# A two-layer diffusion backbone on one core: the context stream goes first in layer 0, and one token tile of the latent stream takes gathered experts there

## The chip, the core and the metric

The kernel runs on one core of a Trainium2 chip. The number that counts is the device time of one execution in microseconds (us). The core has five engines with instruction queues of their own: TensorE (PE in the profile; its weight loads, PEld, overlap its matmuls), VectorE (DVE), ScalarE (ACT), GpSimd (POOL) and SyncE (SP). Each queue runs strictly in its own order. Transfers between main memory and the on-chip buffers are issued from SP, ACT and POOL and share 16 DMA engines.

## The reference

Two layers work on 512 latent tokens (`x`) and 256 context tokens (`ctx`), width 1024. The context goes through the whole of layer 0; in layer 1 only its keys and values are used.

```python
for l in range(DEPTH):                                   # DEPTH = 2
    xn = modulate(rms_norm(h, norm1_g[l]), mod[:, 0], mod[:, 1])
    cn = modulate(rms_norm(hc, norm1_g[l]), mod_c[0], mod_c[1])
    ...
    o = blocked_diff_attn(q, concat([k, kc]), concat([v, vc]), lam)        # x attends to x and ctx
    mix = mixer_output(o, p, ...)                        # gates * (attention, pooling, short conv) @ w_out
    if not last:
        oc = diff_attn_core(qc, kc, vc, lam)             # ctx attends to ctx
        hc = hc + mod_c[2] * mixer_output(oc, pc, ...)
    h = h + mod[:, 2] * mix
    h = h + mod[:, 5] * peer_ffn(modulate(rms_norm(h, ...)), ...)
    if not last:
        hc = hc + mod_c[5] * peer_ffn(modulate(rms_norm(hc, ...)), ...)

def peer_ffn(x, ...):                                    # 16384 experts of one neuron each
    s1, i1 = top_k(scores of the first half key, 16); s2, i2 = top_k(second half, 16)
    top_s, eidx = the best 16 of the 256 sums, for each of 8 heads
    hid = gelu(einsum('td,thkd->thk', x, u_emb[eidx]))
    return einsum('thk,thkd->td', softmax(top_s) * hid, v_emb[eidx])
```

So each token picks 8 x 16 = 128 experts and needs 128 rows of `u_emb` and 128 of `v_emb`.

## The kernel before

A token tile is 128 tokens: `x` has four, `ctx` has two. Float32 products are made of three matmuls on split operands (`mm3`, lines 97 to 100): every weight that arrives from memory is split by ScalarE (line 93) and VectorE (line 94) into a high and a low part. `load_w` brings a projection's weights in pieces of 512 KB (`wraw`, `whi`, `wlo`).

The experts are evaluated in two ways. **Dense**: all 16384 experts for a block of tokens. `hidden` streams the whole of `u` (tiles `uraw`, `uh`, `ul`; 128 of them in a layer, each with 24 matmuls into `hid`), `weigh` multiplies with a gate matrix `G` that `gates` has made (zero where an expert was not picked; `gA`, `gB`, `gE`), and `values` streams the whole of `v` (`vraw`, `vh`, `vl`; again 128 tiles, 24 matmuls each into `dps`, then an addition to `acc`). The matmuls' width is the number of dense tokens. **Gathered**: for one token tile, `gathered` (line 840) fetches the picked rows, one of 128 x 1024 numbers at a time, 256 in all: an indirect DMA issued by POOL (line 846), then one VectorE operation of that size: a dot product with the token's input `gx` for a `u` row (line 859), a weighted addition to `gacc` for a `v` row (line 869). TensorE has no part in it. The rows share a few buffers (tag `row`), so POOL issues the next one when VectorE has used the oldest.

In layer 0 both `ctx` tiles are gathered and all four `x` tiles are dense (width 512); in layer 1 one `x` tile is gathered and three are dense (width 384). `trunk` writes layer 0 in this order: queries, keys and values of both streams (`qkv`), attention of `ctx` and then of `x` (`attend`, `head`), the rest of `ctx` (pooling, convolution, gates, output projection), the pooling of `x`, then `ctx_ffn` with the choice of experts for `ctx` and its gathered rows, and then the rest of `x`. A scheduler at build time sets the order on every engine from the written order and a priority; `prio` shifts it, and the gathered rows carry a shift of 40000, that is, they fill what is left. `head` needs for each head of `x` the loads `hq`, `hk`, `hkl`, `hv`, which POOL's queue issues too, and on VectorE the softmax (`mx`, `at`) and the split `tl` of the transposed weights, on which the matmul into `po` waits.

## Time and profile before

| what | value |
|---|---|
| median of 3 runs | 5148.17 us (5141.2 to 5151.72) |
| the profiled execution, device time | 5138.01 us |
| its span, first to last instruction | 5136.2 us |
| PE busy | 4934.7 us (96%) |
| DVE busy | 3946.9 us (77%) |
| ACT busy | 1988.4 us (39%) |
| POOL busy | 1180.5 us (23%) |
| moved by DMA | 1280.77 MB, mean 249 GB/s |

A share over the whole span is an average of stages with different limits. The profile is therefore read by stretches: for each, how long it took, how much of it each engine was busy, and the share and rate of the DMA engines. In the trace the first gathered row of layer 0 is used at 1092 us, its first dense `u` tile is split at 1335 us, its first `v` tile at 2100 us, its last gathered row at 2953 us, and layer 1's own work begins at about 3010 us.

### The profile page before, as it was taken

What the parts mean: (1) busy time and instruction counts of PE and PEld (TensorE: products, weight loads), DVE (VectorE), ACT (ScalarE), POOL (GpSimd) and SP (SyncE); (2) the same over time, 40 slices, a digit from 0 to 9 for tenths busy, and PEclk for the clock granted to TensorE, in tenths of its full rate; (3) what the DMA queues carried; (4) which work ended last, traced back from release to release, by engine and by line L of the source; (5) the groups of instructions that cost most, each with busy time, mean ns of one, the idle gap of its engine ahead of it and who ended that gap; (6) DMA issues with size and microseconds to landing.
All of it is one profiled execution on the core that took longest, in us unless ns stands there. A gap on an engine that the chain in (4) does not pass through costs nothing.

```text
span 5136.2 us, 73940 instructions
## 1 busy us (share of the span) xinstructions
PE 4934.7 (96%) x27373; PEld 4195.8 (82%) x27373; DVE 3946.9 (77%) x7993; ACT 1988.4 (39%) x2968; POOL 1180.5 (23%) x1028
## 2 busy tenths in 40 slices
PE   8999999998899999989999999999999999899999
PEld 5688787776688788768888789777679999899999
DVE  5457676697899998568888867666359999787885
ACT  4346664422333344222233234544334344332333
POOL 0001000024433343333333300000000434344320
PEclk9999999999999999999999999999999999999999
DMA  8667453468897889999999845533355888988995
GB/s 305 239 200 224 137 191 108 155 200 273 302 316 259 285 312 339 329 321 326 336 341 344 311 137 166 161 126 97 109 172 174 277 309 331 330 314 294 329 317 177
DMA packets 509035, 1280.77 MB, mean 249 GB/s; under 512 B 42496, under 2 KB 224640, under 8 KB 500352
## 3 DMA queue, kind: packets, MB, share of 16 engines
q1 hardware_dynamic: 302816, 669.35, 38.5%
q0 software_dynamic: 131968, 449.90, 25.7%
q10 hardware_dynamic: 73888, 156.79, 8.1%
q8 instruction: 215, 3.52, 0.3%
q14 instruction: 148, 1.21, 0.1%
HBM read 1098.13 MB, written 177.73 MB: 248 GB/s over the span
## 4 chain that ended last, share of the span: by engine, by line
PE 64%; DMA 14%; DVE 11%; issue 7%; POOL 2%; ACT 1%; SPq 0%; ACTq 0%; POOLq 0%; DVEq 0%
PE mm L98 6%; DMA row<-peer_v,ix 6%; PE mm L100 6%; PE mm L99 6%; DMA row<-peer_u,ix 6%; PE dps L99 5%; PE dps L100 5%; PE dps L98 5%; PE hid L100 4%; PE hid L98 4%; PE hid L99 4%; PE qk L98 3%; PE qk L100 3%; PE qk L99 2%; POOL row L846 2%
## 5 line engine op out<-in xcount | busy, mean ns | idle before, releaser
L100 PE MATMUL hid<-yh,ul 128*128 128x512 f32 (+1 forms) x2048 | 760.2, 372 | 33.9 <-DVE ul L94 33.6
L98 PE MATMUL hid<-yh,uh 128*128 128x512 f32 (+1 forms) x2048 | 757.1, 370 | 21.0 <-ACT yh L286 13.2
L846 POOL DMA_INDIRECT row<-peer_v,ix x384 | 568.5, 1480 | 876.7 <-DVE gacc L869 501.1
L846 POOL DMA_INDIRECT row<-peer_u,ix x384 | 521.4, 1358 | 1059.7 <-DVE row L859 617.7
L99 PE MATMUL hid<-yl,uh 128*128 128x512 f32 (+1 forms) x2048 | 755.7, 369 | 2.3 <-DVE yl L287 2.3
L98 PE MATMUL dps<-wh,vh 128*128 128x512 f32 (+1 forms) x2048 | 735.1, 365 | 20.0 <-ACT vh L93 18.6
L99 PE MATMUL dps<-wl,vh 128*128 128x512 f32 (+1 forms) x2048 | 741.7, 365 | 12.3 <-DVE wl L94 12.3
L100 PE MATMUL dps<-wh,vl 128*128 128x512 f32 (+1 forms) x2048 | 742.0, 364 | 10.4 <-DVE vl L94 10.4
L98 PE MATMUL mm<-hi,whi 128*128 128x512 f32 (+1 forms) x1856 | 666.5, 360 | 12.3 <-DVE y L582 3.1
L100 PE MATMUL mm<-hi,wlo 128*128 128x512 f32 (+1 forms) x1856 | 660.6, 358 | 14.0 <-DVE wlo L94 14.0
L99 PE MATMUL mm<-lo,whi 128*128 128x512 f32 (+1 forms) x1856 | 662.4, 357 | 3.5 <-DVE lo L94 3.5
L859 DVE SCALAR_TENSOR_TENSOR row<-row,gx 128x1024 f32<-128x1024 f32 x384 | 467.0, 1221 | 170.3 <-DMA row<-peer_u,ix 169.5
L869 DVE SCALAR_TENSOR_TENSOR gacc<-row,gw,gacc 128x1024 f32<-128x1024 f32 x381 | 488.1, 1281 | 133.7 <-DMA row<-peer_v,ix 132.6
L94 DVE TENSOR_TENSOR wlo<-wraw,whi 128x1024 fp32r<-128x1024 f32 (+1 forms) x356 | 427.2, 1202 | 179.6 <-ACT whi L93 177.2
L93 ACT ACTIVATE uh<-uraw 128x1024 fp32r<-128x1024 f32 x256 | 271.5, 1061 | 716.4 <-PE hid L99 651.9
L93 ACT ACTIVATE whi<-wraw 128x1024 fp32r<-128x1024 f32 (+1 forms) x356 | 370.5, 1043 | 404.4 <-PE mm L99 305.2
L93 ACT ACTIVATE vh<-vraw 128x1024 fp32r<-128x1024 f32 x256 | 270.2, 1058 | 641.9 <-PE dps L99 395.1
L100 PEld LDWEIGHTS hid<-yh,ul 128*128 128x128 f32 x2048 | 390.2, 191 | 82.9 <-DVE ul L94 44.6
L98 PEld LDWEIGHTS hid<-yh,uh 128*128 128x128 f32 x2048 | 391.1, 191 | 64.1 <-ACT yh L286 15.6
L98 PEld LDWEIGHTS dps<-wh,vh 128*128 128x128 f32 x2048 | 386.7, 189 | 61.9 <-ACT vh L93 19.4
L99 PEld LDWEIGHTS dps<-wl,vh 128*128 128x128 f32 x2048 | 387.1, 189 | 54.8 <-DVE wl L94 14.4
L100 PEld LDWEIGHTS dps<-wh,vl 128*128 128x128 f32 x2048 | 387.2, 189 | 51.5 <-DVE vl L94 11.1
(332 smaller groups left out, 9480.4 us busy)
## 6 DMA issues: line engine op xcount, KB each, us to landing
uraw<-uT SPq DMA_DIRECT2D x256, 512.0 KB, 5.7
vraw<-v SPq DMA_DIRECT2D x256, 512.0 KB, 6.8
wraw<-w_in SPq DMA_DIRECT2D x216, 512.0 KB, 4.4
gd<-gst ACTq DMA_DIRECT2D x28, 2048.0 KB, 10.7
mw<-w_mod SPq DMA_DIRECT2D x96, 512.0 KB, 7.0
wraw<-wq SPq DMA_DIRECT2D x80, 512.0 KB, 6.0
hidd<-ge ACTq DMA_DIRECT2D x128, 256.0 KB, 5.6
G<-gd SPq DMA_DIRECT2D x32, 1024.0 KB, 10.7
```

Source lines behind the costliest of these rows:

```text
L93: self.nc.scalar.activation(hi, src, AF.Copy)
L94: self.nc.vector.tensor_tensor(lo, src, hi.bitcast(F32), op=OP.subtract)
L98: mm(ps, lh, rh, start=start, stop=False)
L99: mm(ps, lh, rl, start=False, stop=False)
L100: mm(ps, ll, rh, start=False, stop=stop)
L846: nc.gpsimd.indirect_dma_start(out=r, out_offset=None, in_=a[t], in_offset=bass.IndirectOffsetOnAxis(ap=idx[:, s:s + 1], axis=0))
L859: nc.vector.scalar_tensor_tensor(out=r, in0=r, scalar=1.0, in1=x, op0=OP.mult, op1=OP.mult, accum_out=hid[:, k:k + 1])
L869: nc.vector.scalar_tensor_tensor(acc, r, w[:, k:k + 1], acc, op0=OP.mult, op1=OP.add)
```

## The change

It has five parts.

1. **One tile of `x` is gathered in layer 0 too** (`self.gath = (1, 1)`). The dense block there has 384 tokens instead of 512, three tiles' gate matrices are built instead of four, and 256 more rows are fetched, with a priority of their own (`late[0] = (1000, 28)`: 1000, and 28 more for each row). Their sum goes to memory (`natx`), and `gather_end` transposes and adds it when the dense values are done.
2. **`ctx` first.** `trunk0` writes attention, branches, output projection and expert choice of `ctx` before the attention of `x`. The pooling and convolution of `x` follow its attention.
3. **The rows' sums of `ctx` are added late.** They go to memory (`natc`), and layer 1 (`trunk1`, `begin`) reads them back, adds them, and makes the norm, keys and values of `ctx` after the pooling of `x`. `qkv` is called for `x` and for `ctx` apart, so in layer 1 the weights of keys and values are loaded and split twice (16 pieces of 512 KB more).
4. **Buffers.** Four row buffers instead of three; one instead of two for each of `hv`; five `at` in layer 0 instead of six; two `nt` in a norm with `nat`; the keys in four pieces; three instead of four `vh` and `vl` in the mixed stage of layer 1.
5. The merge of the convolution's output with the gates is a step of its own (`v`, then `o`), and `gx` stays on chip instead of going through memory.

```diff
-    def attend(self, l, es, parts, side=None):
+    def attend(self, l, es, parts, side=None, ahead=2):
...
-                v = [ap_.tile([P, nk, P], F32R, tag=f"hv{x}", name=f"hv{x}") for x in range(2)]
+                v = [ap_.tile([P, nk, P], F32R, tag=f"hv{x}", name=f"hv{x}", bufs=1) for x in range(2)]
...
-            at = ap_.tile([P, nk * P], F32, tag="a", name="at", bufs=6)
+            at = ap_.tile([P, nk * P], F32, tag="a", name="at", bufs=na)
...
-            r = gp.tile([P, D], F32, tag="row", name="row", bufs=3)
+            r = gp.tile([P, D], F32, tag="row", name="row", bufs=self.rows)
...
+                with self.prio(late[0] + n * late[1]):
+                    r = fetch("peer_u", h * 16 + k)
+                    nc.vector.scalar_tensor_tensor(out=r, in0=r, scalar=1.0, in1=x, op0=OP.mult, op1=OP.mult,
+                                                   accum_out=hid[:, k:k + 1])
+                n += 1
...
+    def gather_end(self, l, nat, c, n, i, gp, gq, h):
...
+        nc.sync.dma_start(h, self.hmid[l][:, c:c + n].rearrange("(k p) t -> p k t", p=P))
+        for t in range(n // P):
+            acc = gp.tile([P, D], F32, tag="gend", name="gend", bufs=1)
+            nc.sync.dma_start(acc, nat[t * P:(t + 1) * P, :])
+            self.gather_add(l, acc, i, gq, h[:, :, t * P:(t + 1) * P])
...
+        self.rows = 4
...
+        self.gath, self.late = (1, 1), ((1000, 28), (40000, 0))
...
-            self.qkv(l, [X, Cx], "kqv")
-            if l == 0:
-                self.attend(l, ea, [(Cx, XT, CT), (X, 0, TT)], "right")
-                with ExitStack() as e2:
-                    hc = self.mixers(l, Cx, self.pool(e2, "fc", 2, PSUM), cp, "pcgo")
-                with ExitStack() as e2, self.prio(4000):
-                    self.pooling(l, [X], self.pool(e2, "fp", 2, PSUM))
-                ea.close()
-                ges = self.ctx_ffn(l, hc)
-                ec.close()
-                with ExitStack() as e2:
-                    hm = self.mixers(l, X, self.pool(e2, f"fl{l}", 3, PSUM), xp, "gco")
...
+        self.qkv(0, [X, Cx], "kqv")
+        with ExitStack() as ea, ExitStack() as e2:
+            self.attend(0, ea, [(Cx, XT, CT)], "right")
+            hc = self.mixers(0, Cx, self.pool(e2, "fc", 2, PSUM), cp, "pckvgo")
+        self.ctx_ffn(0, hc, cp, gpools)
+        ec.close()
+        with ExitStack() as ea, ExitStack() as e2:
+            self.attend(0, ea, [(X, 0, TT)], "right", 1)
+            hm = self.mixers(0, X, self.pool(e2, "fl0", 2, PSUM), xp, "pc|kvgo", ea)
...
+        self.qkv(1, [X], "kqv")
...
+        def begin():
+            ges.close()
+            with ExitStack() as ec:
+                self.parts(ec, "xc1", Cx)
+                self.load_norm(1, Cx, lambda h, hp, es: self.gather_end(0, self.natc, NX, NC, 1, hp, self.pool(es, "gq", 1, PSUM), h))
+                self.qkv(1, [Cx], "kv")
+            self.attend(1, ea, [(X, 0, TT)], "right")
...
-        nd = XT if l == 0 else XT - 1
+        nd = XT - self.gath[l]
...
-                        self.values(l, n, cs, self.weigh(l, n, va, cs, had), lambda dq: (vb, 3, vb, EC + 2), vq, acc, c == S + EC)
+                        self.values(l, n, cs, self.weigh(l, n, va, cs, had), lambda dq: (vb, 3, vb, EC + 1), vq, acc, c == S + EC)
```

What the scheduler makes of it is seen in the queues. First VectorE, layer 0, the last head of the attention of `x`; `tl` is the split on which TensorE waits, `row` and `gacc` are gathered rows. Before:

```order
L94 TENSOR_TENSOR tl<-tr_6283,th 128x512
L94 TENSOR_TENSOR wlo<-wraw,whi 128x512
L527 TENSOR_TENSOR psum_9637<-pu 128x527
L527 TENSOR_TENSOR psum_9639<-psum_9637 128x525
L527 TENSOR_TENSOR psum_9641<-psum_9639 128x521
L530 TENSOR_TENSOR psum_9641<-psum_9641,edge 128x4
L532 TENSOR_TENSOR psum_9641<-psum_9641,edge 128x3
L535 SCALAR_TENSOR_TENSOR pd<-psum_9641,pu 128x512
L94 TENSOR_TENSOR pl<-pd,ph 128x512
L94 TENSOR_TENSOR tl<-tr_6295,th 128x512
```

After:

```order
L443 SCALAR_TENSOR_TENSOR at<-p,rcx,at 128x768
L875 SCALAR_TENSOR_TENSOR gacc<-row,gw,gacc 128x1024
L94 TENSOR_TENSOR tl<-tr_11925,th 128x512
L875 SCALAR_TENSOR_TENSOR gacc<-row,gw,gacc 128x1024 x3
L94 TENSOR_TENSOR tl<-tr_11937,th 128x512
L875 SCALAR_TENSOR_TENSOR gacc<-row,gw,gacc 128x1024 x2
L862 SCALAR_TENSOR_TENSOR row,ghid<-row,gx_7555 128x1024
L94 TENSOR_TENSOR tl<-tr_11949,th 128x512
L862 SCALAR_TENSOR_TENSOR row,ghid<-row,gx_7555 128x1024 x3
L94 TENSOR_TENSOR tl<-tr_11961,th 128x512
```

Before, no gathered row stood in the attention; after, three stand ahead of each split.

Second POOL's queue, in the same part of layer 0, the loads for the heads of `x`. Before:

```order
L408 DMA hk<-kd_65 128x1536
L406 DMA hq<-qd_63 128x2x512
L410 DMA hkl<-ld_67 128x768
L413 DMA hv_5116<-vd_69 128x768
L413 DMA hv_5117<-vd_69 128x768
```

After:

```order
L408 DMA hk<-kd_65 128x1536
L406 DMA hq<-qd_63 128x2x512
L410 DMA hkl<-ld_67 128x768
L849 DMA row<-peer_u,ix_8621 128x1024 x16
L849 DMA row<-peer_v,ix_8621 128x1024 x4
L413 DMA hv_10770<-vd_69 128x768
L413 DMA hv_10771<-vd_69 128x768
L849 DMA row<-peer_v,ix_8621 128x1024 x2
```

The fetches of rows and the heads' loads now stand in one another's way.

Third VectorE in layer 0's stage of dense values. Before:

```order
L869 SCALAR_TENSOR_TENSOR gacc<-row,gw,gacc 128x1024
L94 TENSOR_TENSOR vl<-vraw,vh 128x1024
L800 TENSOR_TENSOR gel<-gel,G 128x512 x4
L869 SCALAR_TENSOR_TENSOR gacc<-row,gw,gacc 128x1024
L94 TENSOR_TENSOR vl<-vraw,vh 128x1024
L859 SCALAR_TENSOR_TENSOR row,ghid<-row,gx 128x1024
L94 TENSOR_TENSOR wl<-gel,wh 128x512
L831 TENSOR_TENSOR acc<-dps,acc 128x512
```

After:

```order
L94 TENSOR_TENSOR vl<-vraw,vh 128x1024 x2
L875 SCALAR_TENSOR_TENSOR gacc<-row,gw,gacc 128x1024 x2
L835 TENSOR_TENSOR acc<-dps,acc 128x384
L875 SCALAR_TENSOR_TENSOR gacc<-row,gw,gacc 128x1024 x2
L835 TENSOR_TENSOR acc<-dps,acc 128x384
L875 SCALAR_TENSOR_TENSOR gacc<-row,gw,gacc 128x1024
L94 TENSOR_TENSOR wl<-gel,wh 128x384 x4
L875 SCALAR_TENSOR_TENSOR gacc<-row,gw,gacc 128x1024 x2
```

About two rows go with each value tile in place of one to two, and the other operations are narrower.

## Rows read from the trace of the kernel before

**Rows 1.** The page's head: span, then busy time of each engine
```profile
span 5136.2 us, 73940 instructions
PE 4934.7 (96%) x27373; PEld 4195.8 (82%) x27373; DVE 3946.9 (77%) x7993; ACT 1988.4 (39%) x2968; POOL 1180.5 (23%) x1028
```

**Rows 2.** The page's 40 slices: VectorE's busy tenths, then GB/s moved
```profile
DVE  5457676697899998568888867666359999787885
GB/s 305 239 200 224 137 191 108 155 200 273 302 316 259 285 312 339 329 321 326 336 341 344 311 137 166 161 126 97 109 172 174 277 309 331 330 314 294 329 317 177
```

**Rows 3.** Busy time by stretch: ends, length, engines, clock, DMA share, GB/s
```profile
core 0: us, PE busy (x) PEld busy (x) DVE busy (x) ACT busy (x) POOL busy (x), PEclk, DMA share, GB/s
...
350.00:1092.00 742.00, 723.27 (x4105) 591.07 (x4105) 545.64 (x1406) 399.87 (x657) 60.78 (x160) 0.97 0.52 165
1092.00:1335.00 243.00, 213.89 (x891) 168.39 (x889) 186.65 (x242) 64.43 (x80) 107.62 (x93) 0.98 0.83 282
1335.00:2100.00 765.00, 737.79 (x4346) 615.77 (x4346) 691.28 (x1625) 289.23 (x439) 270.49 (x184) 0.98 0.86 304
2100.00:2953.00 853.00, 826.37 (x3601) 680.15 (x3601) 699.22 (x905) 247.66 (x318) 316.97 (x241) 0.98 0.94 329
2953.00:3010.00 57.00, 50.60 (x196) 36.13 (x195) 35.74 (x57) 21.47 (x35) 0.00 (x0) 0.92 0.53 166
3010.00:5136.00 2126.00, 2048.76 (x11985) 1869.54 (x11984) 1605.92 (x3226) 836.22 (x1241) 420.83 (x339) 0.98 0.66 226
1372.00:1991.00 619.00, 605.13 (x3617) 510.85 (x3618) 587.31 (x1484) 231.19 (x354) 218.37 (x154) 0.99 0.86 300
2600.00:2900.00 300.00, 300.00 (x1324) 248.14 (x1323) 265.19 (x355) 88.75 (x112) 111.24 (x87) 1.00 0.98 343
```

**Rows 4.** The same view for `dps` (512 wide, 384 wide) and `qk` (256 wide)
```profile
2300.00:2900.00 600.00, 600.00 (x2647) 496.61 (x2647) 76.42 (x112) 1.00 0.97 338
4800.00:5100.00 300.00, 298.73 (x1714) 296.27 (x1713) 38.92 (x72) 1.00 0.83 288
3060.00:3200.00 140.00, 133.01 (x1069) 129.21 (x1069) 14.60 (x22) 12.54 (x21) 1.00 0.47 152
```

**Rows 5.** VectorE's groups by line and shape: count, busy us, mean ns, idle before
```profile
L869 DVE SCALAR_TENSOR_TENSOR gacc<-row,gw,gacc 128x1024 f32<-128x1024 f32 x381 | 488.1, 1281 | 133.7 <-DMA row<-peer_v,ix 132.6
L859 DVE SCALAR_TENSOR_TENSOR row<-row,gx 128x1024 f32<-128x1024 f32 x384 | 467.0, 1221 | 170.3 <-DMA row<-peer_u,ix 169.5
...
L94 DVE TENSOR_TENSOR ul<-uraw,uh 128x1024 fp32r<-128x1024 f32 x256 | 311.9, 1219 | 47.6 <-ACT uh L93 47.6
...
L831 DVE TENSOR_TENSOR acc<-dps,acc 128x512 f32<-128x512 f32 x120 | 82.0, 686 | 20.7 <-PE dps L100 20.7
...
L743 DVE TENSOR_TENSOR gB<-gE,sl 128x1024 f16<-128x1024 f16 x112 | 76.7, 686 | 5.4 <-PE gps L751 5.2
...
L831 DVE TENSOR_TENSOR acc<-dps,acc 128x384 f32<-128x384 f32 x120 | 65.9, 554 | 33.0 <-PE dps L100 33.0
```

**Rows 6.** Waits of POOL: line, releaser, us in total, times, longest
```profile
POOL row L846 <- DVE row L859: 773.5, 291, 16.5
...
POOL hv L413 <- PE po L100: 191.3, 19, 48.6
```

**Rows 7.** Timeline at the first rows: a fetch, its use, the buffer's next fetch
```profile
1088.58 1.39 POOL L846 DMA_INDIRECT row<-peer_u,ix  x1 [0.30 <-issue]
...
1095.82 1.23 DVE L859 SCALAR_TENSOR_TENSOR row<-row,gx 128x1024 f32<-128x1024 f32 x1 [1.39 <-DMA row<-peer_u,ix]
...
1097.32 1.21 POOL L846 DMA_INDIRECT row<-peer_u,ix  x1 [2.08 <-DVE row L859]
```

**Rows 8.** All uses of `row`, 1080 to 1335 us and 2100 to 2960 us: landing
```profile
DMA to landing us min/median/max: 4.4/6.1/9.2
...
DMA to landing us min/median/max: 4.1/7.1/11.8
```

More of the change, by code (lines that the diff above doesn't have):

```diff
@@ L213, in rotary @@
         nc.sync.dma_start(rows, bass.AP(tensor=r.tensor, offset=r.offset + 384 * l, ap=[[0, P], [1, 2 * HD]]))
+        gains = [rows[:, off:off + HD] for off in (R_QG, R_KG)]
+        if not turn:
+            return None, None, gains
         cs = pool.tile([P, XT, 2, 32], F32, name="cs")
@@ L224, in rotary @@
                                                g[:, 1 - s][:, None].to_broadcast([P, XT, 32]), op0=OP.mult, op1=OP.mult)
-        gains = [rows[:, off:off + HD] for off in (R_QG, R_KG)]
         return rc, rs, gains
@@ new lines, in gathered @@
+        if end is None:
+            with self.prio(late[0] + n * late[1]):
+                nc.sync.dma_start(out, acc)
+        else:
+            end(acc)
+    def gather_end(self, l, nat, c, n, i, gp, gq, h):
+        nc = self.nc
+        nc.sync.dma_start(h, self.hmid[l][:, c:c + n].rearrange("(k p) t -> p k t", p=P))
[3 more added lines that the diff above has]
+            self.gather_add(l, acc, i, gq, h[:, :, t * P:(t + 1) * P])
@@ L880, in load_norm, with gather_add @@
+    def gather_add(self, l, acc, i, gq, h):
+        tr = gq.tile([P, 4, P], F32, tag="gtr", name="gtr", bufs=1)
+        for k in range(KT):
+            self.nc.tensor.transpose(tr[:, k % 4], acc[:, k * P:(k + 1) * P], self.ident)
+            self.nc.vector.scalar_tensor_tensor(h[:, k], tr[:, k % 4], self.modT[l][:, 40 + k, i:i + 1], h[:, k], op0=OP.mult, op1=OP.add)
+    def load_norm(self, l, s, load, between=None, side=None):
         with ExitStack() as es:
@@ L973, in mixers @@
+    def mixers(self, l, s, pp, xp, order, attn=None, begin=None):
         z, m, gates = Stream(s.o, s.n, s.i), Stream(s.o, s.n, s.i), []
@@ L1013, in gather, with gather_out @@
         nc.vector.tensor_copy(gk, g)
-        dst = self.hout if l == 0 else self.out
-        self.gathered(l, [(rows, ix, gk, self.hmid[l][:, cols], i, dst[:, cols])], gp, gq, self.natd[l], late)
+        self.gathered(x, out, ix, gk, gp, late, end)
+    def gather_out(self, gp, gq, acc, c):
+        col = lambda d: d[:, c].rearrange("(k p) t -> p k t", p=P)
+        h = gp.tile([P, KT, P], F32, tag="row", name="gres", bufs=self.rows)
+        self.nc.sync.dma_start(h, col(self.hmid[DEPTH - 1]))
+        self.gather_add(DEPTH - 1, acc, 0, gq, h)
+        self.nc.sync.dma_start(col(self.out), h)
     def ranks(self, mp):
```

261 lines of the change are left out of this document (128 added, 133 removed).

## The prediction

> **What bounds the kernel now.** I read the page's head first: TensorE is busy 96% of the span, VectorE 77% [rows 1]. That alone says that less TensorE work means less time. The slices say where it may not be so: VectorE and the DMA engines are loaded very unevenly [rows 2]. So I went by stretches [rows 3]. In layer 0 from the first dense tile on, three resources are near full at once: from 1335 to 2100 us VectorE is busy 691 of 765 us, and in its densest part (1372 to 1991) 587 of 619, or 95%; from 2100 to 2953 the DMA engines are at a share of 0.94 and 329 GB/s, in the fullest 300 us at 0.98 and 343 GB/s. In layer 1 (3010 to 5136) the shares are 76% of VectorE and 0.66 of the DMA engines. TensorE sets the pace, but in layer 0 by a small margin. The row fetches use up that margin: VectorE sits 134 and 170 us before the two row operations, nearly always for the row's landing [rows 5], and POOL waits 773 us for VectorE to release a row buffer [rows 6].
>
> **The change, part by part.** The sum is made against the profiled execution: span 5136.2 us, device time 5138.0; the median of the runs is 10 us above that.
>
> TensorE's saving. The 6144 dense matmuls of layer 0 go from 512 to 384 columns. In the stages of pure `dps` work one took 600/2647 = 0.2267 us at 512 and 300/1714 = 0.1750 at 384 [rows 4]. 6144 x 0.0517 = 318 us. If TensorE stayed the bound, that would be the gain.
>
> What it costs. 256 more rows of (488.1 + 467.0)/765 = 1.25 us on VectorE [rows 5] are 320 us. Against that stand narrower operations (554 in place of 686 ns; 128 each of two kinds, and about 128 additions: 51 us) and a quarter of layer 0's gate building (64 operations of 686 ns: 44 us). VectorE gains 225 us of work and TensorE loses 318, all in layer 0. The DMA engines get 256 x 0.524 = 134 MB more and some 34 MB less (gates and hidden values of a fourth tile).
>
> Layer 0 must therefore be summed with all three resources. I count along VectorE's order in the changed kernel, with the mean durations of the groups.
>
> *Until the first gathered row.* Queries, keys and values end at about 350 us as before. Then comes `ctx` alone: 2112 projection matmuls of 256 columns at 0.125 us (between 0.131, which holds some transposes, of [rows 4], and half of 0.2267) are 264 us; its eight heads and norms some 40; the choice of experts and the waits in this chain, which the attention of `x` no longer fills at each step, 100 (no row shows the chain alone; between 50, a little over what 742 us of elapsed time for 723 busy lose [rows 3], and 140). First row at 760 instead of 1092 us.
>
> *Trunk of `x` with rows* (299 of them before the first dense tile is split). VectorE's work other than rows from 350 to 1335 was 546 + 187 - 86 x 1.25 = 625 us [rows 3]; about 300 of it is now ahead of the first row, 310 remain. With 299 x 1.25 = 373 that is 683 us of VectorE for about 505 of TensorE: VectorE bounds. At its best 95% this takes 719 us. A second limit is near: a buffer was fetched at 1088.58, used at 1095.82 and fetched again at 1097.32 [rows 7], 8.74 us for one round, so four buffers give a row every 2.2 us, 299 in 653 us. In bursts, such as three rows ahead of every `tl`, this is the slower one: rows cannot come back to back at 1.25 us. In POOL's queue the loads of `hv` stand between the fetches; with one buffer each waits for the last `po` of the head before, a wait that was up to 48.6 us long with two [rows 6], and behind it wait the next rows, VectorE, and by `tl` TensorE. I add 25 us for both (0 to 130): 745 us.
>
> *Dense hidden stage* (259 rows). From 1335 to 2100 VectorE had 691 us; less 182 rows (227) and a quarter of the gates (44), plus 259 rows (323) and 16 more weight splits of 1.22 us (19): 762 us, at 95% 802. DMA: 0.304 x 765 = 233 MB, plus 77 rows (40) and the 16 weight tiles with what is stored for them (12), less narrower hidden and gate tensors (15): 270 MB, at 340 GB/s 794 us. TensorE needs about 700. I take 800.
>
> *Dense values with rows* (209 rows, by the order done after 105 of the 128 value tiles). From 2100 to 2953 the engines moved 0.329 x 853 = 281 MB; less 34 rows (18), 20 value tiles (10), 16 `u` tiles (13), and 23 for narrower gate and hidden reads: 217 MB. At 340 GB/s that is 638 us, at 343 633. VectorE has 699 - 42 - 24 - 20 - 33 (fewer operations) - 43 (narrower ones) = 537 us, at 95% 565; TensorE 105 x 24 x 0.175 = 441 and the rest of the hidden stage, some 480. The DMA engines bound: 635.
>
> The Trainium skill speaks against this last term: the page "DMA: Bandwidth & Descriptors", section "Bandwidth", has 425 GB/s measured for large loads by a single core. By that 217 MB need 511 us, VectorE's 565 would bound this stage, and the sum would be 70 us less; no stretch here shows more than 344 GB/s [rows 2], so I keep 340.
>
> *Tail.* The last 24 tiles' matmuls, 24 x 24 x 0.175 = 101 us, and 24 to layer 1's own work. `gather_end` for `x` is covered, since its last row stands 23 tiles ahead of the end.
>
> Layer 0: 760 + 745 + 800 + 635 + 125 = 3065 against 3010, so 55 us longer.
>
> Layer 1. TensorE bounds it. 16 more weight splits (20 us of VectorE) lie under a stage where VectorE is two thirds busy; if that cover were gone they would cost 20. The sums of `ctx`, two loads, 16 transposes and 16 small additions, move here from layer 0 and stand beside pooling and convolution of `x`. Three value buffers instead of four and one `hv` may uncover some loads. No row shows these three: 20 us, between -10 (four row buffers let the rows finish earlier) and 60.
>
> 5136 + 55 + 20 = 5211 span, 5213 profiled, and 10 more for the median: **5223 us**, 1.5% slower. Break-even is near: the two middle stages need 683 + 762 = 1445 us of VectorE and get 1545; without loss at all, layer 0 ends about 45 us earlier than before.
>
> **Rivals.**
>
> *A. VectorE and DMA run full* (the other side). In the middle stages VectorE is at 99 to 100% (683 and 762, for DMA 787), values at 343 GB/s, `ctx` chain 730: 730 + 683 + 787 + 633 + 125 = 2958, so -52; layer 1 +0: 5096. It decides from 97% on: 75 us less than my sum is no change, and 1445/0.97 = 1490 gives 55 of them. For it: 618 us at 95% were reached with TensorE equally full, and four buffers let more rows wait ready. Against it: both queues are strictly in order, and the row waits grow where rows are dense.
>
> *B. The transfers aren't at their limit at 343 GB/s.* Then four fetches under way instead of three raise the rate, VectorE bounds the values stage too, and 565 stand there in place of 635: 5223 - 70 = 5153, no change. For it: through all slices the rate follows what is asked for [rows 2]. Against it: the share of 0.98 at that rate [rows 3]. By the page "DMA: Bandwidth & Descriptors" of the Trainium skill, named above, it would go this way.
>
> *C. Rows come no faster than in the first 243 us before*, where 86 took 2.8 us each with VectorE only 77% busy: 299 x 2.8 = 840 in place of 745, and the hidden stage at 90% as before, 845: +140, 5363. Landing takes 6.1 us there, 7.1 in the values stage [rows 8]; a fourth buffer cuts the first limit but not a queue held up by `hv`.
>
> *D. TensorE stays the bound*: 505 + 700 + 480 in place of 2180 is far too much to hide; taken as the whole 318 us, 4830. It would need VectorE to do 683 us of work in 505.
>
> *E. The change doesn't do what it says*: were the rows of `x` or `ctx` placed after layer 0's values, layer 1 would wait. The order has all 768 ahead of the last 23 tiles, so this goes.
>
> **How the numbers follow.** Chances: my forecast (5165 to 5300) 0.44, A 0.24, B 0.12, C 0.16, D 0.04. 0.2% (10 us) is about what a measurement of this kernel can tell from no change. Faster: A and D, 0.28; within 0.2%: most of B, 0.10; slower: the rest, 0.62. The range leaves out D, the lower end of A and the upper of C: 5090 to 5335. The forecast's own range is 5165 to 5300.
>
> **What would show it.** Right: first row of layer 0 used at 730 to 800 us; VectorE over 92% busy from there to the first `v` tiles; DMA at 335 to 345 GB/s through the values; TensorE idle in layer 0 waiting for `tl`, `wlo` or `ul` of VectorE; a layer 0 that ends after 3010. Wrong: rates over 350 GB/s (B), a VectorE at 98% with TensorE at no loss (A), or rows 2.8 us and more apart in the trunk with VectorE waiting for landings (C). If layer 1 lengthens by over 60 us, my sum has missed a wait in `begin`.

## The result and the profile after

The changed kernel takes 5303.1 us (median of 4 runs, 5289.1 to 5313.4) against 5149.9 us of the kernel before beside it: a ratio of 1.0299, 95% interval 1.0268 to 1.033. It is 3% slower; 1.5% were predicted. Its profiled execution has a span of 5311.6 us, 175 us over before's [rows 1]. Some 22 of these 175 us are the choice of executions: this one took 5313.4 us, 10 above its median, and that of before 5138.0, 12 below its own.

The head of the page of the changed kernel, and of its slices VectorE, TensorE's granted clock and the DMA rows:

```profile
PE 4767.6 (90%) x27130; PEld 4182.8 (79%) x27130; DVE 4179.0 (79%) x8346; ACT 1951.6 (37%) x2959; POOL 1532.9 (29%) x1284
...
DVE  5466579988789999988898876566637999888875
...
PEclk9999986896979999988899999899979999999999
DMA  8666546878889899999999844443334689999975
GB/s 308 237 186 188 180 131 216 287 264 289 306 305 334 292 360 347 366 379 363 358 350 353 294 152 156 154 139 111 100 115 168 238 308 332 358 318 332 339 261 177
```

TensorE is busy 4768 us instead of 4935 [rows 1], so 167 us less and not the 318 that narrower matmuls were to save, and it is busy 90% of the span instead of 96%. The clock row shows a part of the reason: it has dips between slices 6 and 12, in the dense stages and in layer 1, where before it had none. VectorE got 232 us more work, as the sum had it (225).

The same by stages (ends, length, busy us of each engine with instruction counts, granted clock, DMA share, GB/s). The stages are those of the prediction: up to the first gathered row, to the first dense tile's split, to the first value tile, to the last row, to layer 1's first `qk`, layer 1:

```profile
350.00:834.00 484.00, 429.30 (x2828) 376.09 (x2827) 337.13 (x1009) 224.96 (x398) 35.90 (x91) 0.88 0.52 163
834.00:1614.00 780.00, 606.68 (x2294) 437.07 (x2293) 664.49 (x986) 249.64 (x369) 400.15 (x365) 0.83 0.84 288
1614.00:2384.00 770.00, 678.26 (x4393) 646.05 (x4394) 737.46 (x1662) 275.19 (x418) 392.05 (x265) 0.96 0.94 347
2384.00:2992.00 608.00, 529.72 (x2817) 511.89 (x2817) 539.58 (x759) 182.10 (x250) 258.06 (x202) 0.94 0.99 355
2992.00:3107.00 115.00, 106.91 (x584) 100.17 (x582) 72.02 (x111) 39.67 (x52) 0.00 (x0) 0.99 0.59 196
3107.00:5311.00 2204.00, 2084.05 (x12025) 1882.88 (x12025) 1649.38 (x3280) 853.51 (x1269) 435.79 (x339) 0.96 0.65 223
```

| stage | predicted us | measured us |
|---|---|---|
| end of qkv (350) to the first row of layer 0 | 410 | 484 |
| trunk of `x` with rows | 745 | 780 |
| dense hidden stage | 800 | 770 |
| dense values with rows | 635 | 608 |
| tail | 125 | 115 |
| layer 1 | 2126 + 20 | 2204 |

Against the sum, the two stages ahead of the dense work are 109 us longer, the three dense ones 67 us shorter, layer 1 is 58 us longer: 100 us, which is the difference of the spans (5311.6 against 5211). Between the medians (5303 against 5223) it is 80.

In the trunk of `x` TensorE sits idle 172 us. Its waits there (line, releaser, us in total, times, longest):

```profile
PE ntr L294 <- ACT nfull L291: 40.6, 8, 17.9
PE mm L98 <- ACT hi L93: 31.7, 1, 31.7
PE po L99 <- DVE tl L94: 27.8, 12, 4.2
PE hrb L494 <- DVE hry L133: 14.4, 1, 14.4
```

These are the norm, the merge ahead of `out_proj`, the attention and the gate: chains that go through VectorE, whose queue holds rows between their steps. In the timeline at the merge one sees such a chain, and what the clock does (start, duration, engine, line, operation, idle time before and its releaser):

```profile
1495.73 1.28 DVE L875 SCALAR_TENSOR_TENSOR gacc<-row,gw,gacc 128x1024 f32<-128x1024 f32 x1 [0.56 <-DMA row<-peer_v,ix]
1496.94 0.68 DVE L611 TENSOR_TENSOR cg<-cg,cq 128x512 f32<-128x512 f32 x1
...
1498.63 1.28 DVE L875 SCALAR_TENSOR_TENSOR gacc<-row,gw,gacc 128x1024 f32<-128x1024 f32 x1
...
1501.31 2.08 PE L98 MATMUL mm<-hi,whi 128*128 128x512 f32 x4 [31.71 <-ACT hi L93]
...
1503.18 0.63 PE L99 MATMUL mm<-lo,whi 128*128 128x512 f32 x1
...
1506.98 0.40 PE L99 MATMUL mm<-lo,whi 128*128 128x512 f32 x1
...
1507.22 0.39 PE L100 MATMUL mm<-hi,wlo 128*128 128x512 f32 x1
```

Eleven row operations, 14 us, stand in the 31.7 us in which TensorE waits; the rest is mostly the chain's own steps and its loads. The granted clock is 0.50 from 1470 to 1501 us, where TensorE does nothing, and still 0.50 from 1502 to 1506.4, where a matmul takes 0.63 us (the lower of its two levels); from 1507 on it is 1.00, and the same matmul takes 0.39 to 0.40. VectorE's waiting for rows, over the whole span, fell from the 170 us (`u` rows) and 134 us (`v` rows) of [rows 5] to 101 and 44 us (busy us, mean ns, then idle before):

```profile
L862 DVE SCALAR_TENSOR_TENSOR row<-row,gx 128x1024 f32<-128x1024 f32 x512 | 619.0, 1218 | 100.7 <-DMA row<-peer_u,ix 99.4
...
L875 DVE SCALAR_TENSOR_TENSOR gacc<-row,gw,gacc 128x1024 f32<-128x1024 f32 x508 | 647.6, 1277 | 43.6 <-DMA row<-peer_v,ix 41.7
```

### The profile page after: what moved, and what is told of

Its sections match the earlier page's. It is cut to its first block, busy times and chain, and to the rows that moved or that the text cites. A ratio compares the mean times of both kernels' runs of the same rounds, so it can differ in the third digit from the quotient of the medians.

```text
span 5311.6 us, 74388 instructions
## 1 busy us (share of the span) xinstructions
PE 4767.6 (90%) x27130; PEld 4182.8 (79%) x27130; DVE 4179.0 (79%) x8346; ACT 1951.6 (37%) x2959; POOL 1532.9 (29%) x1284
## 3 DMA queue, kind: packets, MB, share of 16 engines
q14 instruction: 154, 1.26, 0.1%
## 5 line engine op out<-in xcount | busy, mean ns | idle before, releaser
L849 POOL DMA_INDIRECT row<-peer_v,ix x512 | 750.6, 1466 | 843.5 <-DVE gacc L875 434.8
L849 POOL DMA_INDIRECT row<-peer_u,ix x512 | 690.9, 1349 | 908.7 <-DVE row L862 456.8
L100 PE MATMUL hid<-yh,ul 128*128 128x384 f32 x2048 | 711.4, 349 | 78.0 <-DVE ul L94 77.0
L98 PE MATMUL hid<-yh,uh 128*128 128x384 f32 x2048 | 710.2, 347 | 48.9 <-ACT uh L93 42.7
L98 PE MATMUL dps<-wh,vh 128*128 128x384 f32 x2048 | 690.0, 341 | 42.0 <-ACT vh L93 26.5
L100 PE MATMUL dps<-wh,vl 128*128 128x384 f32 x2048 | 677.1, 342 | 31.6 <-DVE vl L94 31.5
L99 PE MATMUL hid<-yl,uh 128*128 128x384 f32 x2048 | 704.7, 344 | 0.1
L99 PE MATMUL dps<-wl,vh 128*128 128x384 f32 x2048 | 691.2, 340 | 2.7 <-DVE wl L94 2.7
L875 DVE SCALAR_TENSOR_TENSOR gacc<-row,gw,gacc 128x1024 f32<-128x1024 f32 x508 | 647.6, 1277 | 43.6 <-DMA row<-peer_v,ix 41.7
L93 ACT ACTIVATE whi<-wraw 128x1024 fp32r<-128x1024 f32 (+1 forms) x372 | 387.7, 1045 | 478.4 <-PE mm L99 357.1
L98 PEld LDWEIGHTS mm<-hi,whi 128*128 128x128 f32 x1728 | 336.4, 195 | 125.4 <-ACT hi L93 55.4
```

The source lines that it names most:

```text
L93: self.nc.scalar.activation(hi, src, AF.Copy)
L98: mm(ps, lh, rh, start=start, stop=False)
L99: mm(ps, lh, rl, start=False, stop=False)
L100: mm(ps, ll, rh, start=False, stop=stop)
L849: nc.gpsimd.indirect_dma_start(out=r, out_offset=None, in_=a[t], in_offset=bass.IndirectOffsetOnAxis(ap=idx[:, s:s + 1], axis=0))
L875: nc.vector.scalar_tensor_tensor(acc, r, w[:, k:k + 1], acc, op0=OP.mult, op1=OP.add)
```

## The experiments

Every run has the kernel before beside it on the same chip; times are medians, and runs that did not share a chip are compared by their ratios to before. Stage ends are read from the profiled execution of each run.

### The order, the merge, layer 1, VectorE's part

**e_order** takes the tile of `x` out of layer 0 and keeps the new order:

```diff
-        self.gath, self.late = (1, 1), ((1000, 28), (40000, 0))
+        self.gath, self.late = (0, 1), ((1000, 28), (40000, 0))
```

> The changed kernel with its new order, but with no tile of x gathered in layer 0 (four dense tiles of 512 columns, 512 gathered rows of ctx, as before the change). Theory (the order is what costs: ctx alone cannot fill TensorE, and layer 1's trunk is longer because ctx's keys stand ahead of the attention): layer 1's trunk again about 95 us longer than before's 816 us, layer 0's first row at about 830 us, TensorE idle over 150 us between 350 us and the first dense tile; in all 5260 to 5400 us, so that gathering one tile of x is worth between +40 and -100 us on top of it. Rival (the gathered rows of x cost the time: VectorE and DMA full): 5150 to 5230 us, the order costs little, and the changed kernel's 5303 is mostly due to the 256 rows.

5388 us, ratio 1.0481 (1.0455 to 1.0507), as the theory had it. Everything but the tile (the order, layer 1, the buffers) costs 4.8%, and in this order the tile gives back 1.8% (to 1.0299). The first row comes at 829 us, the first dense tile at 1558, layer 1 starts at 3180 and takes 2198 us. Its trunk and its dense part (columns as above):

```profile
829.00:1558.00 729.00, 590.92 (x2237) 424.64 (x2235) 627.83 (x939) 236.53 (x342) 378.92 (x346) 0.85 0.85 293
```
```profile
1558.00:3180.00 1622.00, 1591.52 (x8094) 1321.89 (x8095) 1186.42 (x2248) 543.82 (x761) 367.06 (x230) 0.99 0.74 256
```

The dense part is TensorE's alone, at 98%, and its last row is used at 2410 us, 769 us ahead of layer 1; all that is lost lies ahead of the dense part and in layer 1.

**e_merge** sets conv_out (`v`) behind the attention gate (`g`) again; the strings are `"pckgvo"`, `"pc|kgvo"` and `"pack|gvo"`:

```diff
-            hm = self.mixers(0, X, self.pool(e2, "fl0", 2, PSUM), xp, "pc|kvgo", ea)
+            hm = self.mixers(0, X, self.pool(e2, "fl0", 2, PSUM), xp, "pc|kgvo", ea)
```

> The changed kernel with conv_out set behind the attention gate again, just ahead of the merge, for ctx, x in layer 0 and x in layer 1. Theory (TensorE's gaps at the merge cost what they last: 14.4 + 31.7 us in layer 0, 4.1 + 13.5 in layer 1, 7.5 for ctx): with conv_out's 32 projections there to cover the gate's and the merge's chain, 40 to 70 us less, 5235 to 5265 us. Rival (layer 0 is bound by its rows from 834 us on, so a shorter trunk only moves rows into the hidden stage): layer 0 gains under 15 us, layer 1 some 10, 5275 to 5300 us.

5326 us, ratio 1.0356 (1.0323 to 1.0389): against both theories no gain, and if anything a loss (the intervals of the two kernels touch). The 31.7 us gap is gone and the first dense tile comes 27 us earlier (1585 instead of 1613), but layer 1 starts at 3111 instead of 3107: the dense part takes 1526 us instead of 1494, with 17 more rows in it. A gap that closes in the trunk was not a gain for layer 0 here. Layer 1 took 2219 instead of 2204 us, although its 13.5 us gap went too; why was not settled.

**e_l1both** takes layer 1's qkv of `x` and `ctx` together again and starts the attention behind it:

```diff
-        self.qkv(1, [X], "kqv")
-
-        def begin():
-            ges.close()
-            with ExitStack() as ec:
...
+        ges.close()
+        with ExitStack() as ec:
+            self.parts(ec, "xc1", Cx)
...
+            self.qkv(1, [X, Cx], "kqv")
+        self.attend(1, ea, [(X, 0, TT)], "right")
...
-            hm = self.mixers(1, X, self.pool(e2, "fl1", 2, PSUM), xp, "packv|go", ea, begin)
+            hm = self.mixers(1, X, self.pool(e2, "fl1", 2, PSUM), xp, "pckv|go", ea)
```

> The changed kernel with layer 1's queries, keys and values of x and ctx taken together, as in the kernel before: ctx's sums and norm at the start of layer 1, then qkv of both, the attention of x starting right behind them beside pooling, convolution and conv_out. Theory (layer 1's trunk is 94 us longer because the attention starts only at 3478 us, 371 us after layer 1's first qk, where it started 211 us after it before, so that its last 66 us have no projections beside them): the trunk loses 50 to 90 us, 5215 to 5255 us. Rival (one hv buffer and the moved sums cost the time, wherever they stand): under 20 us less, or more time than the changed kernel since the sums then stand exposed, 5285 to 5330 us.

5249 us, ratio 1.0208 (1.0182 to 1.0235). As the theory had it. Layer 1 takes 2122 us instead of 2204, and starts 17 us later, since the sums of `ctx` now stand ahead of it. How much of the 82 us is the attention's earlier start and how much the 16 loads and splits that are saved was not taken apart. In the changed kernel the first scores come 371 us after the first `qk` (211 before), and when the projections beside the attention have run out its last 66 us look so:

```profile
3478.00:3805.00 327.00, 326.11 (x1358) 239.12 (x1358) 206.02 (x357) 149.69 (x231) 16.97 (x44) 1.00 0.35 111
3805.00:3871.00 66.00, 53.23 (x150) 30.48 (x148) 34.38 (x67) 21.36 (x41) 2.60 (x13) 0.67 0.25 76
```

TensorE has 150 matmuls in these 66 us, 13 us of idle time and a clock of 0.67; in e_l1both the last 91 us of the attention are full:

```profile
3700.00:3791.00 91.00, 91.00 (x403) 71.00 (x403) 43.47 (x67) 43.66 (x59) 2.36 (x13) 1.00 0.29 93
```

**e_narrow** makes each row's operation on 128 of 1024 columns:

```diff
-                        nc.vector.scalar_tensor_tensor(acc, r, w[:, k:k + 1], acc, op0=OP.mult, op1=OP.add)
+                        nc.vector.scalar_tensor_tensor(acc[:, :P], r[:, :P], w[:, k:k + 1], acc[:, :P], op0=OP.mult, op1=OP.add)
```

(and the same for `peer_u`'s rows.)

> The changed kernel with each gathered row's VectorE operation made on 128 of its 1024 columns (so the sums of the gathered experts are left out but for an eighth); all fetches stay whole. Theory (VectorE bounds layer 0's trunk and hidden stage): about 1 us per row is saved, 558 rows of layer 0 stand there; trunk and hidden stage fall from 780 and 770 us to what DMA and TensorE need, 620 to 680 and 700 to 740, the values stage stays at its DMA time; 5050 to 5180 us. Rival (waiting for chains and for landings sets these stages, VectorE's share is only filled time): under 60 us less, 5240 us or more.

5181 us, ratio 1.0072 (1.0047 to 1.0097): 2.3% or 117 us less than the changed kernel by the ratios, at the theory's edge. Trunk, hidden stage, and from the first value matmul to layer 1:

```profile
828.00:1481.00 653.00, 574.22 (x2294) 423.39 (x2294) 392.12 (x944) 247.00 (x368) 309.54 (x338) 0.90 0.90 321
1481.00:2345.00 864.00, 754.17 (x4697) 721.91 (x4695) 539.85 (x1804) 298.66 (x450) 422.78 (x344) 0.93 0.97 366
2345.00:2992.00 647.00, 572.21 (x3097) 556.58 (x3097) 392.02 (x766) 203.71 (x274) 165.45 (x152) 0.94 0.88 315
```

The trunk falls by 126 us, to a length that the theory had given it, so VectorE's time for the rows is what costs there; the gap at the merge falls from 31.7 to 22.3 us and the turns' from 40.6 to 17.9. The hidden stage, which the theory had at 700 to 740 us, doesn't fall (864 us to the first `dps`, 855 before the edit): it holds some 40 more rows, and VectorE is down to 62% while the DMA engines are at a share of 0.97. The dense part as a whole, to layer 1, takes 1511 us instead of 1494: there, VectorE's time for the rows is not the bound by itself. That the DMA engines take its place is read from their share and was not tested.

### The rows of `x`, and the old order

**e_few** leaves 224 of the tile's 256 rows out and starts from e_l1both:

```diff
-        for h in range(8):
+        for h in range(nh):
...
-        self.gathered(x, out, ix, gk, gp, late, end)
+        self.gathered(x, out, ix, gk, gp, late, end, 1 if l == 0 and c < NX else 8)
```

> e_l1both (5249 us) with only the first of eight heads of the gathered tile of x in layer 0 (32 rows instead of 256, so that tile's sums are left out but for an eighth); the dense part stays at 384 columns. Theory (TensorE's saving of 318 us is there but 256 rows take it up): layer 0 ends at 2830 to 2930 us instead of 3124, 4960 to 5060 us, and VectorE, DMA and TensorE all show room. Rival (layer 0 is set by ctx's chain and x's trunk and by dense work, rows of x hardly matter): layer 0 ends after 3040 us, 5165 us and more.

5079 us, ratio 0.9839 (0.982 to 0.9859). The dense part of e_few, and that of e_l1both:

```profile
1617.00:2954.00 1337.00, 1269.36 (x7825) 1231.94 (x7824) 1107.64 (x2226) 499.44 (x729) 359.11 (x243) 0.98 0.83 292
```
```profile
1605.00:3124.00 1519.00, 1324.12 (x7828) 1261.51 (x7826) 1365.26 (x2569) 505.34 (x736) 650.57 (x467) 0.95 0.92 335
```

Against e_order's 1622 us, with as many fetches beside it (230 and 243 instructions on POOL), the narrower block saves 285 us, and TensorE's busy time falls by 322 (1591.5 to 1269.4). The 224 rows take 182 of the 285 back, 0.8 us each. So the saving is there, and the rows take up two thirds of it.

**e_old0** and **e_old1** put layer 0's trunk back into the order of before, on top of e_l1both's layer 1, without and with the tile of `x`. The edit also undoes part 5's merge and gives layer 0 its six `at` again, so what is called the order below holds these two:

```diff
-        with ExitStack() as ea, ExitStack() as e2:
-            self.attend(0, ea, [(Cx, XT, CT)], "right")
-            hc = self.mixers(0, Cx, self.pool(e2, "fc", 2, PSUM), cp, "pckvgo")
...
+        with ExitStack() as ea:
+            self.attend(0, ea, [(Cx, XT, CT), (X, 0, TT)], "right", 1)
+            with ExitStack() as e2:
+                hc = self.mixers(0, Cx, self.pool(e2, "fc", 2, PSUM), cp, "pcgo")
+            with ExitStack() as e2, self.prio(4000):
+                self.pooling(0, [X], self.pool(e2, "fp", 2, PSUM))
+        ges, gpools = self.gather_pools("c0")
...
+            hm = self.mixers(0, X, self.pool(e2, "fl0", 3, PSUM), xp, "gco")
```

> The changed kernel with layer 0's trunk in the order of before (attention of x beside that of ctx, pooling of x beside ctx's branches, then ctx's choice of experts, then the rest of x), no tile of x gathered in layer 0, and layer 1's qkv of x and ctx together as in e_l1both; four row buffers and one hv buffer stay. Theory (ctx ahead of x is what costs layer 0 170 us in e_order): layer 0 ends at 3000 to 3060 us, layer 1 takes 2120 to 2150, in all 5130 to 5200 us. Rival (the small parts, one hv buffer, four row buffers, keys in four pieces, cost it): layer 0 ends after 3100 us, over 5250 us.

> e_old0 with one tile of x gathered in layer 0 as in the changed kernel: the gathering without ctx first. Theory (the rows are a chain of their own, 2.5 to 2.8 us each, whatever else runs): first row at about 1090 us, 768 rows end at 3030 to 3250, layer 0 ends at 3150 to 3330 us, in all 5280 to 5460 us, so that ctx first is needed for the gathering. Rival (rows fit under the dense work at 2.4 us or less, and TensorE's saving pays at once): layer 0 ends before 2980 us, 5060 to 5130 us.

e_old0: 5207 us, ratio 1.0107 (1.0082 to 1.0131), between its two theories: layer 0 ends at 3082 us. e_old1: 5238 us, 1.0168 (1.0147 to 1.019), between its two as well: first row at 1045, last at 3011, one each 2.56 us, and layer 1 starts at 3106 us. The changed kernel has its first row 211 us earlier and starts layer 1 at 3107; e_l1both, with the same layer 1 as e_old1, starts it at 3124. So **ctx first moves the rows forward and the end not at all**. The step for that: from 350 us to the first dense tile the changed kernel needs 1263 us, e_old1 1135, for nearly the same TensorE work (5120 and 5051 matmuls); the dense part gets back 127. From the first `dps` to the last row, e_old1 runs at 380 GB/s:

```profile
2332.00:3010.00 678.00, 550.47 (x2747) 530.99 (x2748) 636.43 (x905) 176.79 (x244) 381.35 (x281) 0.88 1.02 380
```

**e_pool** sets only the pooling of `x` beside `ctx`'s branches (otherwise it is e_l1both):

```diff
+            with self.prio(4000):
+                self.pooling(0, [X], self.pool(e2, "fp", 2, PSUM))
...
+            hm = self.mixers(0, X, self.pool(e2, "fl0", 2, PSUM), xp, "c|kvgo", ea)
```

> e_l1both (5249 us) with the pooling of x set beside ctx's branches in layer 0 at a lower rank, as in the kernel before, and taken out of x's own trunk. Theory (ctx's chain alone leaves TensorE unfilled and at a lower granted clock): pooling's projections go into ctx's waits, the first row comes 0 to 30 us later, the trunk of x gets 40 to 70 us shorter, in all 5195 to 5235 us. Rival (the rows set layer 0's length from the first row on): the first row comes later and the end with it, 5245 to 5285 us.

5316 us, ratio 1.0323 (1.0301 to 1.0345), worse than both. The first row comes 108 us later (938 us), the trunk is 60 us shorter, the last row 40 and layer 0's end 64 us later. TensorE's idle time is no less (59 us ahead of the first row, 193 behind it).

**e_old0R** and **e_old1R** put the buffers of `ctx`'s choice of experts back on the right side:

```diff
-                Y.h = self.pool(e1, f"yc{l}").tile([P, KT, NC], F32R, name="yh")
-                Y.l = cp.tile([P, KT, NC], F32R, tag="lo", name="yl")
+                self.parts(e1, f"yc{l}", Y, "right")
...
-                mp = self.pool(e1, f"pkc{l}", 1)
+                mp = self.pool(e1, f"pkc{l}", 1, side="right")
```

> e_old0 (5207 us) with the buffers of ctx's choice of experts (its second norm, keys, ranks) on the right side of the on-chip memory again, as in the kernel before; on the left side, where the changed kernel has them, the branches of x use the same space afterwards. Theory (that sharing makes x's attention gate wait until ctx's choice is done: in e_old0 its first hss stands 74 us later than in b_r4 and TensorE is busy 62 of the 102 us before 1150): first dense tile at 1370 to 1400 us instead of 1445, 5140 to 5165 us, level with before. Rival (the loss comes from the other small parts): first dense tile after 1425 us, 5190 to 5215 us.

> e_old0R with one tile of x gathered in layer 0, that is e_old1 (5238 us) with the buffers of ctx's choice on the right side. Theory (from the first row on the 768 rows set layer 0's length in the old order: 2.56 us each in e_old1, the last one 95 us ahead of layer 1): a shorter trunk brings nothing, first row at 1045 us, last row at 2980 to 3030, 5205 to 5245 us; the tile costs 60 to 90 us over e_old0R. Rival (TensorE and VectorE set it, rows only fill): the 50 us gained in the trunk stay, 5170 to 5195 us.

e_old0R: 5133 us, ratio 0.9961 (0.9945 to 0.9977): a little faster than before, and the fastest kernel here that leaves nothing out. From 1048 to 1150 us, e_old0 and then e_old0R:

```profile
1048.00:1150.00 102.00, 62.04 (x184) 36.78 (x185) 79.81 (x120) 19.32 (x26) 56.99 (x57) 0.70 0.88 308
```
```profile
1048.00:1150.00 102.00, 96.20 (x394) 74.84 (x393) 92.71 (x138) 29.40 (x36) 51.98 (x52) 0.97 0.85 297
```

In the old order, with shared space on the left, the first `hss` of `x`'s gate comes at 1076.5 us, with its own space at 1012.4; the first dense tile at 1445 and 1380. The edit is worth 1.5%, and no row of before could show it; that the gate waits for the shared space is read from these times and not from a wait in the trace.

e_old1R: 5206 us, ratio 1.0087 (1.0071 to 1.0104). The tile costs 1.26% or 73 us in this order, as the theory had it, though the last row comes later than it said. It stands at 3069 us, 17 us ahead of layer 1: here the rows do set the end, and TensorE waits 177 us in the values stage, 102 of them for the split `vl` on VectorE, which is 92% busy. The dense part:

```profile
1431.00:3086.00 1655.00, 1369.61 (x7827) 1300.33 (x7827) 1535.05 (x2796) 507.56 (x741) 886.31 (x617) 0.91 0.96 355
```

**e_l1R** makes the same edit in e_l1both, where `ctx` comes first.

> e_l1both (5249 us; ctx first, one tile of x gathered) with the buffers of ctx's choice on the right side. Theory (in this order x's attention uses the right side right behind ctx's choice, so that x only trades one sharing for another): first dense tile within 25 us of 1605, 5225 to 5265 us; then the 43 us between e_l1both and e_old1R (5206) belong to ctx first. Rival (left side sharing is what delays x's branches here too): first dense tile before 1570 us, 5190 to 5220 us, level with e_old1R, and ctx first costs nothing.

5283 us, ratio 1.0268 (1.0249 to 1.0287): worse than both, the first dense tile 84 us later (1689). `x`'s attention has its buffers on the right side too, which argues that it now waits for `ctx`'s choice as the gate did on the left; that was not tried by itself. With ctx first the left side was the better one. So the same tile gives back 1.8% with ctx first (e_order) and costs 1.26% in the old order: ctx first makes room for the rows, as meant, but costs more than the room is worth. Without the tile it moves layer 0's end from 3012 us (e_old0R) to 3180 (e_order), with it from 3086 (e_old1R) to 3124 (e_l1both).

### Buffers and the rows' place

**b_r4** is the kernel before with four row buffers in layer 0. **b_hold3** and **b_hold4** are the kernel before, with three and four, and the rows of `ctx` held until `out_proj` of `x` has given its first block:

```diff
-            r = gp.tile([P, D], F32, tag="row", name="row", bufs=3)
+            r = gp.tile([P, D], F32, tag="row", name="row", bufs=4 - l)
```
```diff
+    def release(self, hm):
+        for ix, ixf, go in self.held:
+            self.nc.vector.scalar_tensor_tensor(ix, hm[:, 0, :P], 0.0, ixf, op0=OP.mult, op1=OP.add)
+            go()
```

> The kernel before with four row buffers instead of three in layer 0 and nothing else. Theory (a fourth buffer puts more rows into the trunk of x, where each holds up VectorE ahead of TensorE's next step, and TensorE doesn't get that back later: e_old0's layer 0 is 75 us longer than before's with its first dense tile 96 us later): first dense tile at 1390 to 1450 us instead of 1349, 5170 to 5215 us. Rival (four buffers are free or help, and e_old0's loss comes from its one hv buffer or the other small parts): 5110 to 5155 us.

> The kernel before with ctx's gathered rows in layer 0 held back until the first column block of x's out_proj is done (the row indices are made from it), three buffers. Theory (rows in the trunk cost more than rows beside dense work): first dense tile at 1290 to 1320 us instead of 1349; the 91 rows that stood in the trunk come later, the last one at 3000 to 3100 us, so that layer 1 waits for it, 5130 to 5220 us. Rival (the rows in the trunk cost nothing): first dense tile at 1340 to 1350, 5200 us and more.

> As b_hold3, with four row buffers in layer 0. Theory: first dense tile at 1290 to 1320 us, 512 rows at 2.5 to 3 us each end at 2600 to 2850 us, layer 0 ends at 2950 to 2990 instead of 3008, 5085 to 5130 us: faster than before. Rival (four buffers slow TensorE wherever the rows stand, by VectorE's queue): layer 0 ends at 3040 to 3090 us, 5165 to 5215 us.

b_r4: 5152 us, ratio 1.0016 (0.9995 to 1.0037), no change, as the rival had it. Some 40 more rows stand in the trunk, its end is 35 us later (1384), the last row 190 us earlier (2762), and layer 0 ends at 3010 as before: what the trunk loses comes back where fewer rows stand. b_hold3: 5271 us (1.0236), b_hold4: 5221 us (1.0139). The theory fell: with three buffers the first dense tile comes 25 us earlier (1324) but the last row only at 3120 us, and with four buffers the 512 rows take 3.4 us each and end at 3079 us, so TensorE is idle for 98 us between the first value matmul (2281) and layer 1. Rows in the trunk are not waste: when they are held out of it, the dense stages can't take them all in time.

**e_r3** is e_l1both with `self.rows = 3`, **e_nt4** e_l1both with four `nt` in all norms, **e_hv2** e_old0R with two `hv` buffers in layer 1.

> e_l1both (5249 us) with three row buffers. Theory (with three buffers a row's round of 8 to 10 us gives one row every 2.9 to 3.3 us, 768 of them set layer 0's end): last row at 3060 to 3350 us instead of 2982, 5320 to 5450 us. Rival (rows arrive early enough either way and fewer of them stand in the trunk): last row within 40 us of 2982, first dense tile earlier by 30 us or more, 5205 to 5245 us.

> e_l1both (5249 us) with four buffers of nt in the norms that also turn the rows, as before the change. Theory (two buffers hold TensorE's turns of nfull up: 40 us of TensorE's idle time in layer 0 is ahead of ntr, 13 us in e_order where nothing is turned): 15 to 30 us less, 5218 to 5235 us. Rival (the norm waits for VectorE, whose queue is full of rows, and rows not done there are done later): within 8 us of e_l1both.

> e_old0R (5133 us) with two hv buffers again in layer 1. Theory (one buffer makes po wait for its load in layer 1: its attention ends 459 us after its first sc, 429 before the change): attention ends 20 to 30 us earlier, 10 to 25 us less, 5108 to 5123 us. Rival (the attention is held by its conv_out and gate work on TensorE): within 8 us of e_old0R.

e_r3: 5305 us, ratio 1.0313 (1.0289 to 1.0337). Both halves were there: the first dense tile 35 us earlier, the last row 131 us later (3113), and the second decides. With ctx first and 768 rows the fourth buffer is worth 1%. e_nt4: 5272 us (1.0235), no gain: the wait ahead of `ntr` falls to 24 us but the first dense tile comes at 1604 as in e_l1both (1605). It is 0.3% slower, but the intervals overlap. e_hv2: 5136 us (0.9975, 0.9964 to 0.9986), the same as e_old0R within the intervals: in layer 1 one `hv` buffer costs nothing.

## Why the prediction was right in sign and wrong in size

Three steps of the sum failed. The 100 us for the choice of experts and the waits in `ctx`'s chain measured 172. The trunk of `x`, which "VectorE bounds" at 95% busy, took 780 us for 745 with VectorE at 85%: it waits for landings, and TensorE waits for chains whose steps stand behind rows. And the 20 us for layer 1 measured 78, the larger part of it with an attention that starts late. That the total came no further off is luck: the three dense stages took 67 us less than summed, against 167 more elsewhere.

By ratios, the 2.99% are put together from runs: e_old0R is at -0.39%, the tile of `x` in the old order costs 1.26 (e_old1R), ctx first, with its buffers on the better side, another 1.21 (e_l1both), layer 1's order 0.91. The shares depend on the order in which the parts are added, since the tile and ctx first work on each other (e_order), and their sum is exact only because each is a difference to the one before. The prediction had a price for the first of the three costs, took the second for a gain, and the third for 20 us.

- **TensorE's saving** (318 us): right in size where TensorE sets the pace; between e_order and e_few its busy time in the dense part falls by 322 us and the part by 285.
- **The rows eat it**: right. VectorE's extra work came as summed, 232 us for 225. e_few shows 182 us for 224 rows in the dense part.
- **First row at 760**: 834, outside the 730 to 800 given; the stretch took 484 us in place of 410. The branches with attention took 312 us (264 + 40 in the sum), so they were right. The term of 100 us for the choice and the waits was mis-sized: norm and keys took 107 at a clock of 0.86, the choice 65 at 0.66, 172 together:

```profile
350.00:662.00 312.00, 290.08 (x2163) 273.79 (x2163) 193.54 (x421) 161.63 (x273) 19.69 (x70) 0.94 0.60 184
662.00:769.00 107.00, 92.65 (x531) 73.86 (x529) 82.87 (x300) 48.55 (x99) 6.75 (x12) 0.86 0.46 149
769.00:834.00 65.00, 46.57 (x136) 28.45 (x136) 60.72 (x290) 14.77 (x28) 9.46 (x10) 0.66 0.26 84
```

- **The trunk of `x`, "VectorE bounds" at 95%**: its work was right (664 us for 683, 298 rows for 299), the mechanism wrong. VectorE is 85% busy, not over 92, and 90 us of its waiting is for rows to land, with the chain's next step behind them:

```profile
DVE row L862 <- DMA row<-peer_u,ix: 63.1, 46, 6.5
DVE gacc L875 <- DMA row<-peer_v,ix: 27.3, 23, 3.3
```

TensorE, put at 505 us, was busy 607. Its clock of 0.83 (a mean that counts idle time too), for which no step of the sum had a price, is only a part of that: by the mean durations of the same shapes in the kernel before, its matmuls here are 6% longer, by estimate some 33 us of the 607, and in e_narrow the same 2294 matmuls at a clock of 0.90 are still busy 574. So 505 was too little in itself. From 350 us to the first dense tile, before and after:

```profile
350.00:1349.00 999.00, 943.01 (x5000) 761.13 (x4999) 743.31 (x1665) 469.77 (x745) 171.96 (x256) 0.97 0.60 197
350.00:1613.00 1263.00, 1035.86 (x5120) 813.17 (x5119) 1000.61 (x1992) 474.41 (x767) 436.05 (x455) 0.85 0.72 240
```

TensorE has nearly the work of before, is busy 93 us more (120 more matmuls and the lower clock; the split between them was not measured) and idle 171 us more (227 for 56): 264 us together. The 25 us for one `hv` were not there: POOL waits 9 us for `po` in the trunk.

- **Hidden stage 800**: 770, VectorE 96% busy, as worked out. But e_narrow, with VectorE at 62%, has this stage no shorter, so VectorE was not its only limit.
- **Values 635 at 340 GB/s**: the ceiling was none. The stage ran at 355 GB/s, a slice at 379, e_old1 at 380 over 678 us. Rival B's premise was right, and rates over 350 GB/s were its named sign; what it gave was 27 us here and not 70, since VectorE is 89% busy there and not at its 95. What bounds the stage instead was not shown. The Trainium skill's page "DMA: Bandwidth & Descriptors", section "Bandwidth", has 425 GB/s for large loads by one core. The runs lie between that and the 344 of [rows 2]: 392 GB/s is the highest slice of any of them, in e_narrow.
- **Layer 1 +20**: +78. The step looked at the cost of the moved work and not at who stands behind it. TensorE waits 16 us for the sums (`gtr` for `gend`); the larger part goes with the attention's late start, and e_l1both, where it starts earlier, gives 82 us of layer 1 back.
- **Break-even near**: wrong. It took ctx first as a gain of 330 us on the rows' start. e_old1 shows that, with the tile, this is worth nothing at layer 0's end.
- Of the rivals, A (faster) and D needed full engines and did not come; C's 2.8 us a row were 2.6 in the trunk (780 us, nearer to 745 than to C's 840), with the waits for landings that C named; its hidden stage of 845 did not come; E fell. The sign that the prediction named for a missed wait in `begin`, layer 1 over 60 us longer, is what came.

## What to carry to other kernels

When work is pulled forward, price the stretch that it is pulled out of: TensorE with its waits, and at the clock that the rows show where it sits between chains, and VectorE's queue with the new rows between each chain's steps. An earlier start of a filler is only worth something where the filler sets the end; read that from how far its last item stands ahead of the next stage, as in e_old1R (17 us) against b_r4 (247 us). And when a part is moved behind another, ask which long chain starts later for it, and which of the work that used to run beside that chain will be used up by then.

## What the runs showed of the hardware

TensorE's granted clock was lower where its work had gaps: 0.97 before and 0.85 in the changed kernel between 350 us and the first dense tile with nearly the same work, and at the 31.7 us gap 0.50, through the gap and for matmuls of 0.63 us behind it, then 1.00 with 0.39 to 0.40. A DMA share near 1 is no ceiling on the rate: 0.99 went with 355 GB/s in the changed kernel and 1.02 with 380 in e_old1, where [rows 3] had 0.98 at 343. And where a program puts the buffers of a stage can count as much as the change itself: the side of the on-chip memory for those of `ctx`'s choice was worth 1.5% in one order and cost 0.6% in the other.
